# A hybrid attention and recurrence layer: the rotary key in two passes, and a smaller clearing matmul

## The chip, the cores and the metric

The kernel runs on one core of one Trainium2 chip. The metric is the device time of one execution in microseconds. Three runs of the kernel before gave 794.63, 794.14 and 793.93 us: the median is 794.14 us.

The engines are named as the profile names them: PE is the matrix engine, with PEld for its weight loads; DVE is VectorE, ACT is ScalarE, POOL is GpSimd, and SP issues most of the DMAs. Each works through its own list of instructions in order. The lists are made when the kernel is compiled, by a planner that walks the program in the order in which it is written, gives each instruction a priority by its place (moved by `prio`), and fills an engine with the ready instruction of the highest priority. So an engine's order differs in places from the order in the source.

## The reference

One layer of a diffusion backbone over 512 latent tokens and 256 context tokens, with model width 1024, all in 32-bit floats:

```python
cq, ckv, kpe, hq, hi, hg, ff, fb = split(modulate(rmsnorm(x)) @ w_in)   # for latent and for context tokens
# group A, latent attention: 4 heads, 128 plain and 64 rotary key dimensions, values of 128
k = concat([kn, apply_rope(kpe, cos, sin)])     # latent keys; one rotary key for all heads
k_ctx = concat([kn_c, kpe_c])                   # context keys: the rotary part is not turned
o_a = softmax(q @ k.T / sqrt(192)) @ v
# group B, a gated linear recurrence: 4 heads, two directions, in chunks of 64 tokens
A = where(mask, (q * exp(b - b_ref)) @ (k * exp(b_ref - b)).T, 0)       # inside a chunk
o_b = A @ v + (q * exp(b)) @ S                  # S: the state carried from chunk to chunk
x = x + gt1 * (concat([o_a, rmsnorm(o_b) * silu(hg)]) @ w_out)
x = x + gt2 * swiglu(modulate(rmsnorm(x)))      # then a last rmsnorm
```

`apply_rope` turns pairs of the 64 dimensions that lie 16 apart by an angle per token: each dimension is multiplied by a cosine, and its partner, with a sign, by a sine.

## The kernel before

**Numbers in two halves.** A matmul of two 32-bit float operands is done as three faster passes: each operand is stored as a rounded high half and the rest, a low half, and `mm3` (lines 150, 151 and 152) adds high x high, high x low and low x high in PSUM. Weights come in units of 128 x 1024 (`make_unit`): a DMA into `wf`, a cast by ACT into the high half `wh` (L132), and a subtraction by DVE into the low half `wl` (L133). There are three buffers of each, so a unit's preparation waits until PE has finished with the unit three places ahead. The halves of the normalised input are `hh`, `hl` (latent, 512 columns) and `gh`, `gl` (context, 256 columns).

**Stages.** The kernel first makes the modulation and the normalised input, with the first projection beside it. From about 100 us on come the compressed attention inputs (`mla_pass`), then for each head of the recurrence its query (`hgrn_q`) and two gates (`gates`), 8 contraction steps each through `project`. The recurrence itself (`hgrn_dir` for each head and direction, `hgrn_out` for each head) is written as generators in a list `side`; `tick()` advances the first three of them, from inside the projections, so that their small matmuls stand between the large ones. After the last head comes `mla_kpe`, which projects the rotary key, and then the attention's values (`make_v`), the rotary and plain queries (`make_qr`, `make_q`), the keys (`make_k`), the scores, the softmax and the output projection, and last the feed-forward part, which takes the second half of the time.

**The rotary key.** The weight unit holds its 64 columns twice, the second time with partners exchanged, so that one projection of 128 output rows gives the key and the exchanged key: three passes over 512 and over 256 columns in each of 8 steps. DVE multiplies the first 64 rows by the cosines (L713) and the others by the sines (L714); ACT moves the latter to the first 64 partitions (L715); DVE adds (L716). Then the high half is cast twice by ACT (L719, to both partition halves of `krh`) and the low half is subtracted twice by DVE (L720), apart for context, read from PSUM, and latent, read from `kp`.

**The chunk product.** For each head and direction, `pa` takes the product inside the chunks: a bank of 128 x 512, of which the chunks' diagonal blocks are wanted. One matmul with a weight of zeros clears the whole bank (L549). 16 small ones (L555) with 32 weight columns each, one for each group of 32 key tokens, then add into 64 or 32 columns each, leaving out the half chunks that the mask would remove. DVE copies the bank into `am` under the mask (L559); GpSimd adds the two directions (L592).

PSUM is in eight banks: two tiles `big` of two banks each (projections, `make_v`, scores) and four tiles `sm` of one. `hgrn_out` ends with matmuls into `po` (L598, L604), a norm (L610 on ACT, L614 on DVE) and transposes (L620). The states between chunks are copied by ACT (L581, L584) and chained by DVE (L585) in a low priority.

## Time and profile before

| | us |
|---|---|
| median of three runs | 794.14 |
| the profiled execution | 792.62 |
| its span, first to last instruction | 790.8 |
| PE busy | 768.1 (97%) |
| PE's weight loads | 631.7 (80%) |
| DVE busy | 446.9 (57%) |
| ACT busy | 311.4 (39%) |
| POOL busy | 10.1 (1%) |

The mean granted clock of PE is 0.988. The profile gives one execution. A matmul is shown from its start to a modelled end, and matmuls overlap in the pipeline, so the distance from one start to the next is what one costs in a row of them. In a group, the name before the arrow is the tile that is written and those behind it are read; the figure after the bar is the total in us and the mean in ns. A row of the chain of waits names the time at which a piece of it starts, its length, and the engine, tile and line. A row of waits names who waited, on whom, the total, how often and the longest.

### The profile page before, as it was taken

The numbers are of one execution on the slowest core, as the hardware profiler recorded it, in microseconds if no ns is written. First come the engines' busy times: TensorE is split into PE (matmuls) and PEld (weight loads), VectorE is DVE, ScalarE is ACT, GpSimd is POOL, SyncE is SP. The second block draws the span as 40 slices with busy tenths as digits, with TensorE's granted clock in tenths as the row PEclk, the third lists the DMA queues.
The fourth block names the chain that finished last, engine by engine and source line by source line (L and its number), as shares of the span: only waits on it lengthen the run. The fifth ranks groups of instructions, "written<-read, shape, count | busy, mean of one in ns | idle before, by whom it ended". The sixth has DMA issues, their size and how long they took to land.

```text
span 790.8 us, 10832 instructions
## 1 busy us (share of the span) xinstructions
PE 768.1 (97%) x4342; PEld 631.7 (80%) x4342; DVE 446.9 (57%) x820; ACT 311.4 (39%) x569; POOL 10.1 (1%) x18
## 2 busy tenths in 40 slices
PE   8899999999999989999999999999999999999995
PEld 7568878788887768888999888888888888888885
DVE  5576569839778989985566434432333233223324
ACT  6344246434544577664344223222322222212211
POOL 0000000000000100000000000000000000000000
PEclk8899999999999999999999999999999999999997
DMA  9923723311110022345403343423232323332303
GB/s 332 390 76 134 252 80 108 133 57 55 64 55 28 28 80 90 125 165 181 160 2 100 113 160 133 151 89 107 80 107 82 104 78 96 93 100 80 111 3 107
DMA packets 26706, 88.77 MB, mean 112 GB/s; under 512 B 2976, under 2 KB 5280, under 8 KB 26528
## 3 DMA queue, kind: packets, MB, share of 16 engines
q1 hardware_dynamic: 25568, 87.03, 33.0%
q10 hardware_dynamic: 1088, 1.05, 0.4%
q8 instruction: 34, 0.56, 0.3%
q14 instruction: 16, 0.13, 0.1%
HBM read 85.97 MB, written 2.10 MB: 111 GB/s over the span
## 4 chain that ended last, share of the span: by engine, by line
PE 89%; DVE 7%; ACT 2%; issue 1%; DMA 1%; SPq 0%; DVEq 0%; ACTq 0%
PE big L150 18%; PE big L151 17%; PE big L152 17%; PE sm L150 9%; PE sm L151 9%; PE sm L152 9%; PE big L857 2%; PE sm L604 1%; PE sm L876 1%; PE big L858 1%; PE sm L320 1%; DVE U L585 1%; PE sm L598 1%; DVE acl L309 1%; DVE G L506 1%
## 5 line engine op out<-in xcount | busy, mean ns | idle before, releaser
L133 DVE TENSOR_TENSOR wl<-wf,wh 128x1024 fp32r<-128x1024 f32 (+2 forms) x100 | 119.6, 1196 | 186.3 <-ACT wh L132 186.2
L132 ACT CAST wh<-wf 128x1024 fp32r<-128x1024 f32 (+2 forms) x100 | 102.9, 1029 | 280.3 <-PE big L151 167.6
L150 PE MATMUL big<-h2h,wh 128*128 128x512 f32 (+1 forms) x368 | 140.3, 381 | 0.0
L151 PE MATMUL big<-h2l,wh 128*128 128x512 f32 (+1 forms) x368 | 140.0, 381 | 0.0
L152 PE MATMUL big<-h2h,wl 128*128 128x512 f32 (+1 forms) x368 | 140.0, 381 | 0.0
L151 PEld LDWEIGHTS big<-h2l,wh 128*128 128x128 f32 x368 | 69.2, 188 | 14.6
L150 PEld LDWEIGHTS big<-h2h,wh 128*128 128x128 f32 x368 | 69.2, 188 | 14.4
L152 PEld LDWEIGHTS big<-h2h,wl 128*128 128x128 f32 x368 | 69.2, 188 | 14.4
L150 PE MATMUL sm<-ah,wh 128*128 128x512 f32 (+1 forms) x198 | 73.5, 371 | 0.0
L152 PE MATMUL sm<-ah,wl 128*128 128x512 f32 (+1 forms) x198 | 73.4, 371 | 0.0
L151 PE MATMUL sm<-al,wh 128*128 128x512 f32 (+1 forms) x198 | 73.4, 370 | 0.0
L427 DVE SCALAR_TENSOR_TENSOR wl<-wl,cs 128x1024 f32<-128x1024 f32 x32 | 39.0, 1220 | 33.8 <-DMA wl<-in_wmt_dram 33.8
L150 PE MATMUL big<-wh,hh 128*128 128x512 f32 x96 | 40.2, 422 | 3.3 <-ACT hh L340 1.9
L150 PEld LDWEIGHTS sm<-ah,wh 128*128 128x128 f32 x198 | 37.3, 188 | 7.1
L151 PEld LDWEIGHTS sm<-al,wh 128*128 128x128 f32 x198 | 37.3, 188 | 7.1
L152 PEld LDWEIGHTS sm<-ah,wl 128*128 128x128 f32 x198 | 37.3, 188 | 7.1
L150 PE MATMUL big<-hh,wh 128*128 128x512 f32 x104 | 42.8, 412 | 0.0
L151 PE MATMUL big<-hl,wh 128*128 128x512 f32 x104 | 40.9, 394 | 0.0
L152 PE MATMUL big<-hh,wl 128*128 128x512 f32 x104 | 40.8, 392 | 0.0
L151 PE MATMUL big<-wl,hh 128*128 128x512 f32 x96 | 38.8, 406 | 0.0
L152 PE MATMUL big<-wh,hl 128*128 128x512 f32 x96 | 38.4, 402 | 0.0
L506 DVE RECIPROCAL G<-S 128x528 f32<-128x528 f32 x8 | 27.5, 3432 | 0.1
(326 smaller groups left out, 1353.4 us busy)
## 6 DMA issues: line engine op xcount, KB each, us to landing
wf<-in_wgu_dram SPq DMA_DIRECT2D x44, 512.0 KB, 3.4
wl<-in_wmt_dram SPq DMA_DIRECT2D x32, 512.0 KB, 3.5
wf<-in_wi_dram SPq DMA_DIRECT2D x25, 512.0 KB, 3.9
wf<-in_wd_dram SPq DMA_DIRECT2D x16, 512.0 KB, 3.5
wms<-in_wm_dram SPq DMA_DIRECT2D x11, 512.0 KB, 9.6
wf<-in_wo_dram SPq DMA_DIRECT2D x8, 512.0 KB, 3.5
wf<-in_wd_dram SPq DMA_DIRECT2D x8, 384.0 KB, 3.1
wm<-in_wm_dram SPq DMA_DIRECT2D x5, 512.0 KB, 10.2
```

The lines of the kernel that those rows point to most:

```text
L132: nc.scalar.copy(hi[:, :w], f[:, :w])
L133: nc.vector.tensor_sub(lo[:, :w], f[:, :w], hi[:, :w].bitcast(F32))
L150: nc.tensor.matmul(o, lh, rh, start=start, stop=False, skip_group_check=True)
L151: nc.tensor.matmul(o, lh, rl, start=False, stop=False, skip_group_check=True)
L152: nc.tensor.matmul(o, ll, rh, start=False, stop=stop, skip_group_check=True)
L309: nc.vector.tensor_add(acc_, acc_, sq_)
L320: nc.tensor.matmul(ps[32 * g : 32 * g + 32, :256], csil[:, 4 * j + kk, :], f[:, kk * 256 : (kk + 1) * 256], start=(j == 0), stop=(j == 1), ...
L427: nc.vector.scalar_tensor_tensor(f, f, 1.0, sc, op0=ALU.mult, op1=ALU.mult, accum_out=acc)
L506: nc.vector.reciprocal(I, S)
L585: nc.vector.scalar_tensor_tensor(U[:, c1, :], U[:, c0, :], er[:, 1, c0 : c0 + 1], U[:, c1, :], op0=ALU.mult, op1=ALU.add)
L598: nc.tensor.matmul(t, a2[:, j, :], vt[:, j, h * P : (h + 1) * P], start=True, stop=False, skip_group_check=True)
L857: nc.tensor.matmul(ps[:, 0, :], L, R[:, :NL], start=(i == 0), stop=(i == 4), skip_group_check=True)
```

## The change

**The rotary key** is projected from a unit with only its 64 columns, half as wide (512 instead of 1024 columns for each partition). The unit's high half and low half are written side by side into one tile, 64 columns of each for every contraction step, so that one pass gives the product with the high half in the first 64 output rows and with the low half in the other 64. There are two passes for each step, with the high and the low half of the input; the product of the two low halves, which was left out before, is now in the sum. Afterwards ACT moves the lower 64 rows to the first 64 partitions, DVE adds them over all 768 columns, exchanges the partners by a shuffle, and multiplies and adds; casts and subtractions then take latent and context columns together. The tile `kp` uses the buffers of `kk` instead of those of `q`.

**The chunk product** is no longer cleared as a whole. Two matmuls of zeros in bfloat16, with 32 weight columns and 128 moving columns, clear only the corners of the diagonal blocks that the small matmuls don't write; the small matmuls now write instead of adding. The masked copy is done in two operations of 64 partitions, for the diagonal blocks alone.

```diff
-        units.append(("wi", wi[u], UNIT))
+        units.append(("wi", wi[u], UNIT) if u < NW_IN - 1 else ("kp", wi[u][:, : UNIT // 2], UNIT // 2))
...
-        nc.scalar.copy(hi[:, :w], f[:, :w])
-        nc.vector.tensor_sub(lo[:, :w], f[:, :w], hi[:, :w].bitcast(F32))
+        if kind == "kp":
+            f3 = f[:, :w].rearrange("p (k c) -> p k c", c=64)
+            h3 = hi.rearrange("p (k s c) -> p k s c", s=2, c=64)
+            nc.scalar.copy(h3[:, :, 0], f3)
+            nc.vector.tensor_sub(h3[:, :, 1], f3, h3[:, :, 0].bitcast(F32))
+        else:
+            nc.scalar.copy(hi[:, :w], f[:, :w])
+            nc.vector.tensor_sub(lo[:, :w], f[:, :w], hi[:, :w].bitcast(F32))
...
-    zr = HG.tile([P, P], F32R, name="zr")
-    nc.gpsimd.memset(zr.bitcast(F32), 0.0)
+    zr = HG.tile([P, P], F32, name="zr")
+    nc.gpsimd.memset(zr, 0.0)
     zc = zr.bitcast(BF16)
...
         pa = sm()
-        nc.tensor.matmul(pa, zr, hh[:, 0, :], start=True, stop=False, skip_group_check=True)
+        for g in (1 - d, 3 - d):
+            c0 = (g // 2) * CH + 32 * d
+            nc.tensor.matmul(pa[32 * g : 32 * g + 32].rearrange("p (j t) -> p j t", t=P)[:, :, c0 : c0 + 32],
+                             zc[:, 0:32], zc[:, 0:P].rearrange("p (j t) -> p j t", t=32), start=True, stop=True,
+                             skip_group_check=True, tile_position=(0, 32 * g))
...
-                                 start=False, stop=True, skip_group_check=True, tile_position=(0, 32 * g))
+                                 start=True, stop=True, skip_group_check=True, tile_position=(0, 32 * g))
         with prio(100):
             p4 = pa.rearrange("p (j t) -> p j t", t=P)
-            nc.vector.copy_predicated(am[d], mk[:, d : d + 1, :].to_broadcast([P, 4, P]), p4)
+            for g in range(2):
+                r = slice(g * CH, (g + 1) * CH)
+                nc.vector.copy_predicated(am[d][r, :, r], mk[r, d : d + 1, r].to_broadcast([CH, 4, CH]), p4[r, :, r])
...
     def mla_kpe():
-        ps = project(KPU)
-        kp = HG.tile([P, NL], F32, tag="q", name=nm("kp"), bufs=2)
-        m = HG.tile([P, NL], F32, tag="sg", name=nm("kpm"), bufs=2)
-        nc.vector.tensor_mul(kp[0:64, :], ps[0:64, :NL], C("cos")[0:64, :])
-        nc.vector.tensor_mul(kp[64:128, :], ps[64:128, :NL], C("sin")[64:128, :])
-        nc.scalar.copy(m[0:64, :], kp[64:128, :])
-        nc.vector.tensor_add(kp[0:64, :], kp[0:64, :], m[0:64, :])
-        for src, c in ((ps[0:64, NL:NT], slice(NL, NT)), (kp[0:64, :], slice(0, NL))):
-            for r in (slice(0, 64), slice(64, 128)):
-                nc.scalar.copy(krh[r, c], src)
-                nc.vector.tensor_sub(krl[r, c], src, krh[0:64, c].bitcast(F32))
+        w, _ = unit(KPU)
+        ps = big()
+        for k in range(KT):
+            for i in range(2):
+                for o, n, t in ((ps[:, 0, :], NL, (hh, hl)), (ps[:, 1, :NC], NC, (gh, gl))):
+                    nc.tensor.matmul(o, w[:, k * P : (k + 1) * P], t[i][:, k, :n], start=(k == 0 and i == 0),
+                                     stop=(k == KT - 1 and i == 1), skip_group_check=True)
+            if k in (1, 4):
+                tick()
+        ps = ps.rearrange("p a b -> p (a b)")
+        kp = HG.tile([P, NT], F32, tag="kk", name=nm("kp"), bufs=3)
+        m = HG.tile([P, NT], F32, tag="sg", name=nm("kpm"), bufs=2)
+        nc.scalar.copy(m[0:64, :], ps[64:128, :NT])
+        nc.vector.tensor_add(kp[0:64, :], ps[0:64, :NT], m[0:64, :])
+        nc.vector.stream_shuffle(m[0:64, :NL], kp[0:64, :NL], SWAP)
+        nc.vector.tensor_mul(kp[0:64, :NL], kp[0:64, :NL], C("cos")[0:64, :])
+        nc.vector.tensor_mul(m[0:64, :NL], m[0:64, :NL], C("sin")[0:64, :])
+        nc.vector.tensor_add(kp[0:64, :NL], kp[0:64, :NL], m[0:64, :NL])
+        for r in (slice(0, 64), slice(64, 128)):
+            nc.scalar.copy(krh[r, :], kp[0:64, :])
+            nc.vector.tensor_sub(krl[r, :], kp[0:64, :], krh[0:64, :].bitcast(F32))
```

The host packs the last unit with the 64 columns alone and zeros behind them; a second definition of the shuffle's table is dropped.

6 lines of the change are left out of this document (2 added, 4 removed).

## The prediction

> **What bounds the kernel now.** I read the page's first part, then the stretches, the waits of TensorE (PE), the chain of waits, and the timeline of the place where the rotary key is made.
>
> ```profile
> PE 768.1 (97%) x4342; PEld 631.7 (80%) x4342; DVE 446.9 (57%) x820; ACT 311.4 (39%) x569; POOL 10.1 (1%) x18
> ```
>
> Read alone, this row says that every matmul taken out is time won. The stretches say where this isn't so (columns: PE, weight loads, VectorE, ScalarE and GpSimd busy, clock, DMA).
>
> ```profile
> 210.00:230.00 20.00, 20.00 (x156) 16.43 (x155) 17.04 (x41) 8.12 (x19) 0.00 (x0) 1.00 0.09 29
> 264.00:276.00 12.00, 10.35 (x84) 7.75 (x83) 11.64 (x22) 7.51 (x18) 3.57 (x4) 1.00 0.13 46
> 288.00:300.00 12.00, 9.85 (x50) 7.64 (x50) 11.09 (x22) 11.25 (x17) 0.00 (x0) 1.00 0.24 82
> 360.00:400.00 40.00, 40.00 (x250) 35.89 (x249) 21.69 (x37) 16.16 (x26) 0.00 (x0) 1.00 0.40 130
> ```
>
> Up to 230 us and from 360 us on PE never rests, so a shift is kept to the end. Where the rotary key lies, around 264 to 300 us, VectorE (DVE) is nearly full (11.64 of 12) and PE has holes. The longest of PE's waits there, and the chain, name them:
>
> ```profile
> PE big L150 <- DVE krl L720: 1.6, 1, 1.6
> ```
>
> ```profile
> 231.76 1.05 ACT wh L132
> ...
> 237.35 0.62 DVE am L559
> ...
> 251.44 0.70 DVE qg L531
> ...
> 264.97 0.59 DVE kp L713
> ...
> 270.96 0.50 PE big L150
> ...
> 281.92 0.37 PE sm L604 x4
> ...
> 293.51 0.30 PE sm L620
> ```
>
> From 251.44 to 270.96 us the chain is DVE's alone; PE restarts at 270.96 when DVE has read the rotary key's PSUM for the last time (L720). Then PE leads to the last head's output (L604), whose transposes (L620) follow at 293.51.
>
> **The change: PE's part of the rotary key.** One step of its contraction, and a clearing matmul behind it:
>
> ```profile
> 252.88 0.40 PE L150 MATMUL big<-hh,wh 128*128 128x512 f32 x1
> 253.11 0.40 PE L151 MATMUL big<-hl,wh 128*128 128x512 f32 x1
> ...
> 253.58 0.28 PE L150 MATMUL big<-gh,wh 128*128 128x256 f32 x1
> 253.70 0.28 PE L151 MATMUL big<-gl,wh 128*128 128x256 f32 x1
> ...
> 253.93 0.39 PE L549 MATMUL sm<-hh,zr 128*128 128x512 f32 x1
> 254.25 0.65 PE L555 MATMUL sm<-qt,kk 128*32 128x64 f32 x32
> 254.83 0.50 PE L150 MATMUL big<-hh,wh 128*128 128x512 f32 x1
> 255.17 0.39 PE L151 MATMUL big<-hl,wh 128*128 128x512 f32 x1
> ```
>
> Matmuls overlap, so the price is the distance between starts: 0.23 us for a pass over 512 latent columns, 0.12 for 256 context columns, 1.05 for the step of three passes. Two passes leave out one of each in eight steps: 8 x 0.35 = 2.8 us of PE. The weight's own preparation (half the load, half a cast, half a subtraction) falls in the stretch from 210 to 230 us, where PE's other projections keep it busy 20.00 of 20.00 us; I cost it at nothing. Without that cover it would gain half of such a subtraction, 0.6 us by the row of L133 further down.
>
> **The clearing.** L549 takes 0.32 us to the next start here. After other small matmuls it takes more:
>
> ```profile
> 227.09 0.60 PE L544 MATMUL sm<-cs,kk 128*128 128x128 f32 x4
> 227.44 0.47 PE L549 MATMUL sm<-hh,zr 128*128 128x512 f32 x1
> 227.85 0.65 PE L555 MATMUL sm<-qt,kk 128*32 128x64 f32 x32
> ```
>
> That is 0.41 us. What replaces it, two bfloat16 matmuls with 32 weight columns over 128 moving columns, is in no row. From below, L555: 32 records in 0.58 us, so 0.04 for two. From above, a matmul right behind one of another kind: 254.83 to 255.17 is 0.34 where 0.23 is usual; two of those are 0.68. The nearest row is L544, 128 columns, four in 0.35: 0.18 for two. With fewer weight columns I take 0.15, an estimate. Saved: about 0.25 each (from 0.37 down to a loss of 0.27), 2.0 for all eight. Five come before 231.76, where the chain leaves PE for ScalarE (ACT) and DVE: 1.25 us. The sixth is beside the chain; the last two lie in DVE's stretch. The accumulating matmuls that now start afresh have the same shapes: nothing.
>
> By the Trainium skill, "TensorE: Matmul & The Clock Gate", section "Back-to-back issue gap", 128 columns are 134 cycles, 0.056 us, and matmuls in different column groups overlap; each clearing would then save 0.35 and the first five 1.75 instead of 1.25. No run here shows it yet.
>
> **VectorE.** The groups, shapes kept apart (mean ns last before the bar):
>
> ```profile
> L713 DVE TENSOR_TENSOR kp<-big,cs 64x512 f32<-64x512 f32 x1 | 0.7, 675 | 0.0
> L714 DVE TENSOR_TENSOR kp<-big,cs 64x512 f32<-64x512 f32 x1 | 0.7, 694 | 0.0
> L716 DVE TENSOR_TENSOR kp<-kp,kpm 64x512 f32<-64x512 f32 x1 | 1.4, 1416 | 0.0
> L720 DVE TENSOR_TENSOR krl<-big,krh 64x256 fp32r<-64x256 f32 x2 | 0.8, 412 | 0.0
> L720 DVE TENSOR_TENSOR krl<-kp,krh 64x512 fp32r<-64x512 f32 x2 | 1.4, 685 | 0.0
> L786 DVE STREAM_SHUFFLE m<-sm 128x512 f32<-128x512 f32 x2 | 1.5, 732 | 0.0
> L861 DVE TENSOR_REDUCE ast<-big 128x1 f32<-128x768 f32 x1 | 1.0, 958 | 0.4 <-PE big L858 0.4
> L559 DVE COPY_PREDICATED am<-mk,sm 128x512 f32<-128x512 int32 x8 | 5.7, 710 | 0.0
> ```
>
> The rotary key costs DVE 0.68 + 0.69 + 1.42 + 2 x 0.41 + 2 x 0.69 = 4.98 us. Afterwards: one add over 768 columns (0.96, as L861), a shuffle (0.73), two products and an add over 512 (3 x 0.69), two subtractions over 768 (2 x 0.96): 5.68. The masked copy becomes two of 256 columns at about 0.41 each (as L720): 0.13 more each time, once on the chain at 237.35 and twice behind it. So DVE's list between 251 and 297 us grows by 0.70 + 0.26 = 0.96 us. The 1.42 of L716 is twice what its size asks (L714: 0.69). It ran beside this row:
>
> ```profile
> 267.18 1.27 POOL L592 TENSOR_TENSOR a<-am,am 128x512 f32<-128x512 f32 x1 [27.58 <-DVE am L559]
> ```
>
> GpSimd's add ends at 268.45 and L716 at 269.00. I credited the removal of the whole 1.42, so if one of the new operations meets that add, up to 1.27 comes on top: from 0 to 1.27, I take 0.35, half the excess seen.
>
> The Trainium skill, "SBUF — State Buffer", section "SBUF: two separate sides", says a DVE operation with two SBUF inputs and a GpSimd operation that reads SBUF exclude each other for a whole instruction; it speaks against this change, whose products and last add are all of that kind. L716 bears it out: blocked to 268.45, then 0.55. By the rule alone the list grows by 0.96 + 0.73 = 1.69.
>
> **ScalarE.** The rotary key took five copies, three over 512 columns (0.62, first row) and two over 256, at most 3.1 us. Now there are three over 768, 0.81 each by the sigmoid of that size:
>
> ```profile
> 269.03 0.62 ACT L719 CAST krh<-kp 64x512 fp32r<-64x512 f32 x1 [1.36 <-DVE kp L716]
> 270.58 0.27 ACT L581 COPY U<-sm 128x128 f32<-128x128 f32 x1
> L470 ACT ACTIVATE sg<-big 128x768 f32<-128x768 f32 x8 | 6.4, 806 | 0.0
> ```
>
> 2.4 us; the gain of up to 0.7 is on an engine busy 7.51 of 12 us and costs or gives nothing. The new first copy makes DVE's add wait; queued behind it is DVE's whole list, but PE delivers 2.8 us sooner, so the copy finds ACT and PSUM ready by the time DVE reaches L713's place at 264.97.
>
> **Where the stall goes.** The key's PSUM is now read out by that one add, some 5 us ahead of 270.96, so PE's 1.64 us wait at 270.96 goes. What is late next is DVE's list up to the last head's states (for L604, 281.92) and to the `ow` that L620 transposes. DVE's own gaps from 279 to 297 are
>
> ```profile
> 278.99 0.69 DVE L803 TENSOR_TENSOR vl<-big,vh 128x512 fp32r<-128x512 f32 x1 [0.56 <-ACT vh L802]
> 281.18 1.23 DVE L133 TENSOR_TENSOR wl<-wf,wh 128x1024 fp32r<-128x1024 f32 x1 [0.38 <-ACT wh L132]
> 287.01 0.17 DVE L191 TENSOR_SCALAR rsv<-oss 128x4 f32<-128x4 f32 x1 [0.46 <-ACT osq L610]
> 287.50 0.69 DVE L776 SCALAR_TENSOR_TENSOR qnl<-big,qnh 128x512 fp32r<-128x512 f32 x1 [0.32 <-ACT qnh L775]
> ```
>
> 1.72 us, all behind work that waits for PE; a PE some 4 us ahead can close them. A weight subtraction like the one at 281.18, 1.23 us, can also be left until after the first scores; I count half of it, 0.6.
>
> **Sum.** -1.25 (five clearings) + 0.13 (masked copy on the chain) = -1.12 at 251.44. Then +0.96 + 0.35 (DVE's list) - 1.72 (gaps) - 0.6 = -1.01. Together -2.1 us: the profiled execution goes from 792.62 (790.8 of span and 1.8 around it) to 790.5. The median of the three runs is 794.14, 1.5 above the profiled one; on it the forecast is **792.0**. Of 4.8 us of PE work removed, less than half arrives.
>
> **Rivals.**
> 1. *All of PE's saving arrives.* For it: PE's 97%, and the instruction order is planned anew, so DVE's less urgent work may move past 300 us. Against: DVE 11.64 of 12 us busy from 264 to 276. -4.8: 789.3.
> 2. *DVE swallows the key's saving.* The gaps stay, because all four rows name ACT as what ended them, the block recurs in full: -1.12 + 0.96 + 0.73 = +0.6, less half a subtraction left until later (0.6) and 0.2 of the gaps: -0.2, so 793.9. For it: the chain is DVE's from 251 to 271. Against: the copies that ACT waited on come from PE, which is now ahead.
> 3. *Slower: the states queue behind the longer key.* On ACT the casts of the key stood at 269.03, ahead of the states' copy at 270.58, in order. From L713's place at 264.97 the new chain needs 0.96 + 0.73 + 3 x 0.69 = 3.8 us, with masked copies (0.82) and a full block (1.27) 2.1 more: 270.9 instead of 269.0. With two casts 0.19 longer each the states start 2.3 later; less the 1.12, +1.2: 795.3. It decides once the new last add ends over 1.12 us after 269.0 and PE has nothing else to put before L604. Against: the planner can issue the states first.
> 4. *The change doesn't do what it says:* if the corner pair cost 0.68, five clearings lose 1.35; it moves forecast and rival 2 up by 2.6. I count it within rivals 2 and 3.
>
> **Numbers.** Forecast 0.50, own range 790.8 to 793.2 (clearing 0.1 to 0.35 each, block 0 to 1.27); all of PE 0.17; swallowed 0.23; slower 0.10. A change below 0.2%, 1.6 us, can't be told from none: the line lies at 792.55. Forecast gives four fifths to faster, rival 1 all: 0.57. Slower, beyond 795.7, is a little under half of rival 3 and the tail of rival 2: 0.06. The rest, 0.37, is same. The range runs from rival 1's price to just under rival 3's: 789.3 to 794.9.
>
> **What would show it.** Right: 16 matmuls fewer of L150 to L152's kind in the key, its span from 8.4 to 5.6 us of matmuls; the clearing pair at about 0.15 us; no PE wait of 1.6 us on the key's PSUM; DVE still over 95% busy from 264 to 276; L620 at about 291.4. Wrong: L620 near 289 (rival 1) or at 293 and later (rival 2), the states' first copy on ACT after 271 (rival 3), or a clearing pair at 0.4 us or more.

## The result, and the profile after

The changed kernel takes 800.81 us (median of 4 runs, 799.62 to 801.84) against 794.05 of the kernel before: ratio 1.0083, 95% interval 1.0065 to 1.0101. It is slower, by some 6.8 us, where 2.1 us less were forecast. The profiled execution took 799.62 us, with a span of 797.8.

Line numbers shift: L150 to L152 are now L156 to L158, the states' links L585 are L597, the weighted heads L614 are L626, their transposes L620 are L632, the first scores L857 are L877. First the row of busy times from the page's first part, and TensorE's longest waits around the rotary key, with one from further up, on `shg` (total, times, longest):

```profile
PE 766.2 (96%) x4334; PEld 629.3 (79%) x4334; DVE 450.7 (56%) x829; ACT 311.9 (39%) x567; POOL 10.7 (1%) x18
```

```profile
PE sm L632 <- DVE ow L626: 5.3, 1, 5.3
PE big L877 <- ACT pp L883: 2.5, 1, 2.5
PE sm L156 <- ACT U L596: 1.8, 1, 1.8
...
PE big L156 <- DVE shg L650: 1.0, 1, 1.0
...
PE big L156 <- DVE kp L733: 0.9, 1, 0.9
```

PE lost exactly the instructions it was to lose (4342 - 16 key passes + 8 second corner matmuls = 4334), and the 1.6 us wait on the key's PSUM fell to 0.9. But PE now waits 5.3 us for the last head's weighted heads, where it waited 1.2 us in the kernel before, and 2.5 us for the first exponentials.

Four marks divide the span: the decayed queries `qg` of the last head's first direction (the queries times their decay, `q * exp(b)` of the reference), the weighted heads `ow` (the last head's output under its norm and gate), the first scores, the end. For the kernel before, two of them had no row yet (timeline: start, duration, engine, line, operation):

```profile
293.02 1.12 DVE L614 SCALAR_TENSOR_TENSOR ow<-sm,rsr,shg 128x128 f32<-128x128 f32 x4
296.80 0.39 PE L857 MATMUL big<-knh,qnh 128*128 128x512 f32 x1
```

and for the changed kernel:

```profile
250.71 0.69 DVE L537 TENSOR_TENSOR qg<-qt,S 128x512 f32<-128x512 f32 x1 [2.74 <-PE sm L616]
295.65 1.13 DVE L626 SCALAR_TENSOR_TENSOR ow<-sm,rsr,shg 128x128 f32<-128x128 f32 x4
301.97 0.40 PE L877 MATMUL big<-knh,qnh 128*128 128x512 f32 x1
```

| stretch, us | before | after | difference |
|---|---|---|---|
| start to `qg` | 251.44 | 250.71 | -0.73 |
| `qg` to `ow` | 41.58 | 44.94 | +3.36 |
| `ow` to first scores | 3.78 | 6.32 | +2.54 |
| first scores to the end of the span | 494.0 | 495.8 | +1.8 |

All of the loss lies behind `qg`. The 0.73 us before it are not the change's. The transposes in front of the first clearing, up to which both kernels do the same work, already start 1.06 us apart (before, then changed):

```profile
129.33 0.38 PE L539 MATMUL sm<-cs,kk 128*128 128x128 f32 x2
128.27 0.38 PE L545 MATMUL sm<-cs,kk 128*128 128x128 f32 x2
```

In the first 60 us the profile of the kernel before has a granted clock of 0.91, that of the changed kernel 0.94: 10.2 and 6.8 us at half clock. Two profiles in which the order is the old one up to here, before and before_sqrt_late further down, differ in the same way: 10.2 and 3.4 us at half clock, and the first clearing at 129.91 and 128.22. From these transposes to `qg` the changed kernel took 122.44 us, the kernel before 122.11.

**From `qg` to `ow`.** VectorE's timeline of the changed kernel, from the key's first add (L733) to the last link of the states (L597):

```profile
262.66 0.95 DVE L733 TENSOR_TENSOR kp<-big,kpm 64x768 f32<-64x768 f32 x1
...
266.35 0.90 DVE L571 COPY_PREDICATED am<-mk,sm 64x256 f32<-64x256 int32 x2 [1.06 <-PE sm L565]
267.28 0.68 DVE L735 TENSOR_TENSOR kp<-kp,cs 64x512 f32<-64x512 f32 x1
267.89 1.77 DVE L736 TENSOR_TENSOR kpm<-kpm,cs 64x512 f32<-64x512 f32 x1
...
272.09 1.91 DVE L740 TENSOR_TENSOR krl<-kp,krh 64x768 fp32r<-64x768 f32 x2
...
275.89 1.21 DVE L139 TENSOR_TENSOR wl<-wf,wh 128x1024 fp32r<-128x1024 f32 x1
...
282.04 0.68 DVE L796 SCALAR_TENSOR_TENSOR qnl<-big,qnh 128x512 fp32r<-128x512 f32 x1
...
285.01 0.33 DVE L597 SCALAR_TENSOR_TENSOR U<-U,er 128x128 f32<-128x128 f32 x1
```

In the kernel before, the key's last subtractions and the last link of the states were these:

```profile
270.94 1.38 DVE L720 TENSOR_TENSOR krl<-kp,krh 64x512 fp32r<-64x512 f32 x2
...
280.46 0.35 DVE L585 SCALAR_TENSOR_TENSOR U<-U,er 128x128 f32<-128x128 f32 x1
```

GpSimd's row beside L736 in the changed kernel:

```profile
267.42 1.69 POOL L604 TENSOR_TENSOR a<-am,am 128x512 f32<-128x512 f32 x1 [28.53 <-DVE am L571]
```

The last link of the states ends at 285.34, 34.6 us after `qg`; in the kernel before it ended at 280.81, 29.4 us after. Of these 5.3 us, 2.4 are there when the key is done: its last subtraction ends 23.3 us after `qg`, in the kernel before 20.9. There the key's longer work on VectorE and the wait of 1.06 us up to 266.35 count. The other 2.9 us come behind the key, from the order. Ten links stand in the list there, each a third of a microsecond, where the kernel before had eight, and between them stand a weight subtraction, value and query splits (the subtractions that make the low halves `vl`, `qnl`) and rotary products; in the kernel before, the weight subtraction came behind the last link and no query split in front of it. PE's parts of these end sooner in the planned order, which presumably is why the planner put them in front of links that decide more.

**From `ow` to the scores, and behind.** The stretches (PE, weight loads, VectorE, ScalarE and GpSimd busy, clock, DMA):

```profile
292.00:294.00 2.00, 0.00 (x0) 0.00 (x0) 1.53 (x3) 1.97 (x4) 0.00 (x0) 0.78 0.74 236
294.00:296.00 2.00, 0.00 (x0) 0.00 (x0) 1.90 (x7) 1.97 (x4) 0.00 (x0) 0.50 0.86 258
296.00:298.00 2.00, 1.85 (x7) 1.59 (x8) 1.76 (x5) 1.96 (x3) 0.00 (x0) 0.50 0.22 82
298.00:300.00 2.00, 2.00 (x8) 1.61 (x7) 1.94 (x3) 1.97 (x4) 0.00 (x0) 0.52 0.00 0
300.00:304.00 4.00, 4.00 (x25) 3.51 (x24) 2.51 (x6) 2.56 (x5) 0.00 (x0) 1.00 0.45 131
...
310.00:312.00 2.00, 2.00 (x12) 1.86 (x10) 1.78 (x6) 0.69 (x3) 0.00 (x0) 0.54 0.46 121
312.00:314.00 2.00, 2.00 (x9) 1.76 (x8) 1.54 (x5) 1.77 (x5) 0.00 (x0) 0.60 0.37 141
```

During the 5.3 us wait the granted clock falls to one half. A stretch of 2 us at clock c holds (1 - c) x 4 us of half clock: 0.88 + 2 + 2 + 1.92 = 6.8 us, then 1.84 + 1.60 = 3.4 us after the wait for the exponentials. The kernel before has none between 240 and 340 us:

```profile
240.00:340.00 100.00, 94.52 (x623) 76.65 (x623) 90.20 (x186) 65.62 (x143) 3.57 (x4) 1.00 0.23 76
```

PE worked from 296.15 (the end of the wait) to about 299.9 at half clock, which loses it half of 3.8 us, and through the second fall, half of 3.4: 1.9 and 1.7 us of PE's work. The second is nearly all of the +1.8; how much of the +2.54 the first is, these rows don't say.

ScalarE adds a piece: the square root that is meant to warm its table for the end of the kernel (L1057) had been planned this early, and in the changed order its table load stands ahead of the casts of the nope key (`knh`, the plain part of the keys, which is not turned):

```profile
299.74 1.28 ACT L1057 ACT_TABLE_LOAD   x1
...
301.14 1.50 ACT L788 CAST knh<-sm 128x512 fp32r<-128x512 f32 x3
...
306.36 1.28 ACT L883 ACT_TABLE_LOAD   x1 [3.72 <-DVE ast L881]
```

In the kernel before the first nope-key casts started at 296.06 and this load at 297.88, behind them.

### The profile page after: what moved, and what is told of

It reads as the page before. It is cut to its first block, busy times and chain, and to the rows that moved or that the text cites. A ratio compares the mean times of both kernels' runs of the same rounds, so it can differ in the third digit from the quotient of the medians.

```text
span 797.8 us, 10824 instructions
## 1 busy us (share of the span) xinstructions
PE 766.2 (96%) x4334; PEld 629.3 (79%) x4334; DVE 450.7 (56%) x829; ACT 311.9 (39%) x567; POOL 10.7 (1%) x18
## 4 chain that ended last, share of the span: by engine, by line
PE 80%; DVE 9%; DMA 5%; ACT 3%; issue 2%; SPq 0%; DVEq 0%; ACTq 0%
PE big L156 16%; PE big L157 15%; PE big L158 15%; PE sm L156 9%; PE sm L157 9%; PE sm L158 9%; PE big L877 2%; DMA wl<-in_wmt_dram 1%; DMA xc<-in_ctxT_dram 1%; PE sm L896 1%; PE sm L616 1%; DVE wl L139 1%; DMA wm<-in_wm_dram 1%; DMA wms<-in_wm_dram 1%; PE big L878 1%
## 5 line engine op out<-in xcount | busy, mean ns | idle before, releaser
L139 DVE TENSOR_TENSOR wl<-wf,wh 128x1024 fp32r<-128x1024 f32 (+1 forms) x99 | 118.4, 1196 | 186.6 <-ACT wh L138 186.5
L138 ACT CAST wh<-wf 128x1024 fp32r<-128x1024 f32 (+1 forms) x99 | 101.8, 1029 | 276.5 <-PE big L157 162.5
L156 PE MATMUL big<-h2h,wh 128*128 128x512 f32 (+1 forms) x368 | 140.3, 381 | 0.0
L158 PE MATMUL big<-h2h,wl 128*128 128x512 f32 (+1 forms) x368 | 140.0, 381 | 0.0
L158 PEld LDWEIGHTS big<-h2h,wl 128*128 128x128 f32 x368 | 69.2, 188 | 14.4
L156 PEld LDWEIGHTS big<-h2h,wh 128*128 128x128 f32 x368 | 69.2, 188 | 14.4
L156 PE MATMUL sm<-ah,wh 128*128 128x512 f32 (+1 forms) x198 | 73.5, 371 | 0.0
L158 PE MATMUL sm<-ah,wl 128*128 128x512 f32 (+1 forms) x198 | 73.4, 371 | 0.0
L156 PE MATMUL big<-wh,hh 128*128 128x512 f32 x96 | 39.4, 414 | 4.3 <-ACT hh L346 1.9
L156 PEld LDWEIGHTS sm<-ah,wh 128*128 128x128 f32 x198 | 37.3, 188 | 7.1
L158 PEld LDWEIGHTS sm<-ah,wl 128*128 128x128 f32 x198 | 37.3, 188 | 7.1
L156 PE MATMUL big<-hh,wh 128*128 128x512 f32 x96 | 39.4, 410 | 0.0
L158 PE MATMUL big<-wh,hl 128*128 128x512 f32 x96 | 38.2, 399 | 0.0
L157 PE MATMUL big<-hl,wh 128*128 128x512 f32 x96 | 37.8, 394 | 0.0
L158 PE MATMUL big<-hh,wl 128*128 128x512 f32 x96 | 37.7, 393 | 0.0
L156 PEld LDWEIGHTS big<-wh,hh 128*128 128x128 f32 x96 | 17.9, 188 | 12.5 <-ACT hh L346 3.6
```

What stands on the lines that cost most here:

```text
L138: nc.scalar.copy(hi[:, :w], f[:, :w])
L139: nc.vector.tensor_sub(lo[:, :w], f[:, :w], hi[:, :w].bitcast(F32))
L156: nc.tensor.matmul(o, lh, rh, start=start, stop=False, skip_group_check=True)
L157: nc.tensor.matmul(o, lh, rl, start=False, stop=False, skip_group_check=True)
L158: nc.tensor.matmul(o, ll, rh, start=False, stop=stop, skip_group_check=True)
```

## The experiments

Theory A, formed from this profile: the last head's chain, threaded through queues in the planner's order, sets this stretch; the change altered that order for the worse, and PE's saving became waits. Rival, called C further on: the new parts cost by themselves, whatever the order. The letters of the expectations are not always these: for clear_only and key_only, A is the key's longer work and B the order; for the two runs with the late square root, A is that table loads lie on the chain and B that they hide in waits. All ratios are to the kernel before, run on the same chip beside it. The last three columns are read from one profiled execution each, as above.

| kernel | ratio (95%) | `qg` to `ow` | `ow` to scores | half clock, 240 to 340 |
|---|---|---|---|---|
| before | 1 | 41.6 | 3.8 | 0 |
| the whole change | 1.0083 (1.0065 to 1.0101) | 44.9 | 6.3 | 10.2 |
| clear_only | 1.0013 (0.9993 to 1.0033) | 41.8 | 6.0 | 3.4 |
| key_only | 1.0056 (1.0034 to 1.0078) | 42.4 | 7.1 | 6.8 |
| two_passes_old_chain | 1.0115 (1.0086 to 1.0143) | 42.8 | 9.3 | 10.2 |
| three_passes_new_chain | 1.0066 (1.0031 to 1.0101) | 42.7 | 7.3 | 6.8 |
| states_first | 1.0054 (1.0034 to 1.0075) | 41.3 | 6.8 | 6.8 |
| before_states_first | 1.0065 (1.0033 to 1.0097) | 43.4 | 7.8 | 6.8 |
| key_after_head1 | 1.0157 (1.0133 to 1.0181) | 42.5 | 6.0 | 13.6 |
| filled_wait | 1.0055 (1.0036 to 1.0075) | 44.9 | 4.6 | 3.4 |
| after_sqrt_late | 1.0055 (1.0028 to 1.0081) | 44.9 | 4.7 | 3.4 |
| before_sqrt_late | 1.0003 (0.9979 to 1.0027) | 41.6 | 3.8 | 0 |
| chain_first | 1.0072 (1.0045 to 1.0098) | 34.8 | 14.9 | 3.4 |
| before_chain_first | 1.0043 (1.0020 to 1.0066) | 37.7 | 10.3 | 3.4 |
| loads_late | 1.0168 (1.0134 to 1.0202) | 46.3 | 4.6 | 6.8 |
| before_loads_late | 1.0103 (1.0081 to 1.0125) | 41.6 | 3.2 | 0 |
| chain_first_loads_late | 1.0112 (1.0087 to 1.0136) | 38.7 | 11.3 | 10.2 |
| before_chain_first_loads_late | 1.0093 (1.0061 to 1.0124) | 37.7 | 6.5 | 0 |
| filled_sqrt_late | 1.0054 (1.0032 to 1.0076) | 46.3 | 4.6 | 3.4 |
| filled_sqrt_late_states_mid | 1.0041 (1.0017 to 1.0065) | 42.2 | 7.0 | 3.4 |

**One part alone.** clear_only is the kernel before with the diff's parts in `hgrn_dir` and `zr`; key_only the kernel before with all the others.

> Only the corner clearing and the two masked copies; the rotary key as before. Theory A (the loss comes from the key: its longer work on VectorE and ScalarE holds up the last head's states): the clearing saves about 0.2 us each, so 792 to 793.5 us, PE waits for ow about 1.2 us as before. Theory B (any change of PE's pace makes the planner put the last head's states later on VectorE): slower than before, 795 to 799, with a PE wait for ow of over 3 us.

> Only the rotary key in two passes; the old clearing of the whole bank. Theory A: 800 to 802.5 us, the whole loss and 1 us of clearing more, PE waits about 5 us for ow. Theory B: slower too, but by any amount between 796 and 802, since the planner's order is another one again.

Clearing alone makes no difference that can be measured, though PE waits 2.6 us for `ow` with it (1.2 before), which neither expectation had; the key alone costs 0.56%, with a wait of 4.7 us, inside B's range and under A's. GpSimd's block did not recur in key_only, so the key is slower without it too (the product that took 1.77 us above):

```profile
270.17 0.76 DVE L729 TENSOR_TENSOR kp<-kp,cs 64x512 f32<-64x512 f32 x1
270.86 0.68 DVE L730 TENSOR_TENSOR kpm<-kpm,cs 64x512 f32<-64x512 f32 x1
```

Then the key's two halves, PE's passes and VectorE's chain, each without the other:

```diff
 two_passes_old_chain, against before (with the new clearing)
-        ps = project(KPU)
...
+            for i in range(2):   # hh x wh and hl x wh, hh x wl left out
+                for o, n, t in ((ps[:, 0, :], NL, (hh, hl)), (ps[:, 1, :NC], NC, (gh, gl))):
+                    nc.tensor.matmul(o, L[0], t[i][:, k, :n], ...)
...
 three_passes_new_chain, against the whole change
-            for i in range(2):
+            for i in (0, 1, 1):
```

> The new clearing, the old weight layout and the old VectorE work for the rotary key, but only two of its three passes (the product of the input's high half with the weight's low half is left out): PE's saving alone. If the longer VectorE work is the cause of the loss: 791.5 to 793.5. If PE's saving itself turns into a wait, with a halved clock behind it: 795 to 799, with PE waiting for ow over 3 us.

> The whole change with a third pass in the rotary key (the input's low half counted twice): VectorE's new work alone, PE as before. If the longer VectorE work is the cause: 799 to 802. If it takes PE's saving to bring about the loss: 793 to 796.

Both are slower than before, and the one with PE's saving and the old, shorter VectorE chain is likely the slower of the two (the intervals overlap a little). PE's saving by itself brought no gain: it came back as waits of 2.6 us for the third head's `ow`, 2.8 for the nope key and 2.2 for the exponentials, with 10.2 us of half clock. Its median of 803.3 is above both expectations. The other run, with 798.5, lies just under the 799 to 802 that were given for VectorE's longer work as the cause: the new chain, beside a PE that has as much to do in the key as before, is enough for most of the loss. That speaks for C; but the order is another one there too.

**The order alone.** The links of the last head's states have priority -100 in the planner; states_first and before_states_first make it +100, in the changed kernel and in the kernel before:

```diff
-        with prio(-100):
+        with prio(100 if h == NH - 1 else -100):
             U = HG.tile([P, NCH, P], F32, tag="U", name=nm("U"), bufs=2)
```

> The whole change, and the last head's state chain (ScalarE's copies and VectorE's links) planned 100 places earlier instead of 100 later. If the states' place in the queues is the cause: no PE wait for ow above 2 us, the last head's output matmuls start before 281 us instead of at 285.8, no clock below 0.95 between 288 and 300 us, 789 to 792.5 us. If it is the amount of work on VectorE (rotary key 5.7 us and the block by GpSimd): the wait moves to another place and the time stays at 798 to 801.

> The kernel before with the same priority for the last head's states and nothing else. If the states' place is the cause of the loss only in the changed kernel: 792.5 to 794.5, since they stood well there already. If the old kernel lost time by it too (its waits of 1.6 and 1.2 us): 790 to 792.5.

With the priority the states ended 23.3 us after `qg` in the changed kernel, 11.3 us sooner, and `ow` came only 3.6 us sooner: PE's output products stood behind value products in PE's order. The time stayed at 799.5 and the waits moved (1.8 us for `onl`, 2.2 for the exponentials), which is what was expected if the amount of VectorE's work is the cause. The same one-line edit makes the kernel before 0.65% slower with nothing else changed, against both of its expectations. So an order alone, with the same work, moves the time by nearly as much as this change did. That is the strongest row for theory A. key_after_head1 moves the key out of the stretch (and its weight unit with it):

```diff
...
-    mla_kpe()
+        if h == 1:
+            mla_kpe()
+            tick()
     tick()
```

> The whole change, and the rotary key projected after the second head (its weight unit moved in the list), where VectorE has slack, instead of after the last one. If the amount of work that VectorE has between 251 and 300 us sets the time: that stretch (from the last head's qg to the first scores, 45.4 us before, 51.3 in the changed kernel) falls to 40 to 43 us plus nothing elsewhere, 788 to 791.5 us. If it is only the order that the planner happens to choose: the stretch minus PE's key work stays over 43, and the time is anywhere from 793 to 800.

It is the slowest but one, and its time lies outside both expectations (the stretch to the scores is 48.5 us). Without the key PE has less to do beside the last head's chain; it waits 6.4 us for `ow` and 5.3 us for a value split and has four windows of half clock. `qg` to `ow` stays at 42.5: work taken from PE here is not time won.

**The clock.** In filled_wait PE multiplies 128 x 128 ones (22 products) in the wait for `ow`; no result uses them, and the order of the instructions up to there is that of the changed kernel.

```diff
+        rr0 = sq
...
         pt = sm()
+        if h == NH - 1:
+            with prio(0):
+                for _ in range(22):
+                    nc.tensor.matmul(pt[:, :P], ones, rr0, start=True, stop=True, skip_group_check=True)
         for j in range(4):
             nc.tensor.transpose(pt[:, j * P : (j + 1) * P], w[:, j, :], ident)
```

> The whole change, with 22 idle matmuls (ones times an old tile, the result overwritten) put in front of the last head's transposes, where PE waited 5.3 us for ow. The engines' orders are those of the changed kernel up to that place, so the wait itself stays. If PE's halved clock after the wait is part of the loss: clock 1.00 from 290 to 300 us, passes 0.23 us apart instead of 0.43 behind the transposes, the first scores 1.5 to 2 us earlier than in the changed kernel, 798.5 to 799.5. If the slow clock costs nothing because ScalarE and VectorE set the pace there: 800 to 801.5.

```profile
288.00:300.00 12.00, 11.73 (x82) 10.03 (x83) 10.47 (x21) 11.12 (x22) 0.00 (x0) 1.00 0.38 132
300.00:320.00 20.00, 17.87 (x103) 15.77 (x102) 15.48 (x31) 13.29 (x26) 0.00 (x0) 0.91 0.26 80
```

The clock stays at 1.00 through the wait, `ow` to scores falls from 6.3 to 4.6 us, and the ratio from 1.0083 to 1.0055; the intervals of the two ratios overlap. The fall behind the first scores stays (0.91). But the clock is not all that changed. Behind the fillers the planner put the square root's table load behind the nope key's casts, where the changed kernel had it in front:

```profile
298.89 1.37 ACT L793 CAST knh<-sm 128x512 fp32r<-128x512 f32 x3
300.28 1.28 ACT L1062 ACT_TABLE_LOAD   x1
```

So this run can't say what the half clock in the wait was worth: the 1.7 us may be the load's. The next run, after_sqrt_late, takes the load out and keeps 3.2 us of half clock behind the wait, and its first scores come nearly as soon after `ow` (4.7 us). What it loses is other work of PE: up to the first scores it has done 6 passes over 512 columns of the key projection, filled_wait 12, a difference of 1.4 us at 0.23 each.

The mean granted clock of every run is on record, and says more than one profile. The ten runs of filled_wait have 0.9886 on average, those of the kernel before beside them 0.9879, and filled_wait is still 4.5 us slower on average: that much is lost without any more half clock than the kernel before has. In key_only the means are 0.9830 and 0.9879. Within the runs of the kernel before, 0.01 of clock goes with 7 to 8 us, so the clock would be some 3.8 of key_only's 5.0 us, and with 0.9848 against 0.988 some 2.5 of the changed kernel's 6.8; both are estimates.

**Table loads.** Two runs make the warm-up square root read the last tile of the feed-forward product, so that it can't be planned early:

```diff
-    nc.scalar.activation(epst2, epst, AF.Sqrt)
+    nc.scalar.activation(epst2, al[:, FT - 1, 0:1].bitcast(F32), AF.Sqrt, scale=0.0, bias=epst)
```

> The whole change; the square root that warms its table for the end of the kernel (L1057) reads the last tile of the feed-forward product, so that its 1.28 us table load and the reload of the exponential's table leave the stretch ahead of the first scores. Computes the same result. Theory A (loads on the chain): the first nope-key casts no longer stand behind the load at 299.74, and the exponential no longer behind a reload; last weighted heads to first scores 6.3 -> about 4.5 us, time 800.8 -> 797 to 798.5. Still slower than before, because the states' detour (44.9 us from the last decayed queries to the weighted heads, against 41.6) stays. Theory B (loads hide in waits): no difference over 0.5 us.

> The kernel before with the same late square root. Theory A: before has its load behind the first nope-key cast, so only the exponential's reload goes, 1.3 us at most: 792.5 to 793.7 beside 794.0. Theory B: no difference. With the run above it says how much of the 6.8 us is the place of a table load: the difference of the two gains, 1 to 3 us by A, 0 by B.

In the changed kernel the casts now follow the output's copy at once and the reload of the exponential's table is gone:

```profile
299.05 0.67 ACT L634 ACTIVATE onh<-sm,vc 128x512 fp32r<-128x512 f32 x1
299.69 1.08 ACT L788 CAST knh<-sm 128x512 fp32r<-128x512 f32 x2
304.70 0.90 ACT L883 ACTIVATE pp<-big,ast 128x768 f32<-128x768 f32 x1 [3.93 <-DVE ast L881]
```

Scores 1.6 us sooner, the first exponential 3.0 us sooner (304.70 against 307.65), and the wait that had halved the clock a second time is gone. 1.0055 instead of 1.0083, as expected; the intervals overlap here too. In the kernel before the profile has the first exponential 1.3 us sooner after `qg` (49.2 us against 50.5), which the times, at 0.9979 to 1.0027, can't show.

**The whole chain ahead.** chain_first gives priority +100 not only to the states but to the last head's output products, norm, weighted heads and transposes, with the late square root; before_chain_first does the same to the kernel before.

```diff
+        with prio(100 if h == NH - 1 else 0):
             po = sm()
             for j in range(4):
             ...
+        with prio(100 if h == NH - 1 else 0):
             pt = sm()
             for j in range(4):
                 nc.tensor.transpose(pt[:, j * P : (j + 1) * P], w[:, j, :], ident)
             ...
```

> The whole change with the late square root, and the last head's states, output products, norm, weighted heads and their transposes given priority in the planner (+100), so that the tail of this head no longer stands behind the value and query splits of the attention in VectorE's and TensorE's queues. Computes the same result. Theory A (the last head's chain in the planner's order sets this stretch, and the change lengthened it): the weighted heads come before the last query products, at 33 to 38 us after the last decayed queries instead of 44.9; TensorE then has no wait over 2 us up to the first scores and no half clock, so the stretch to the first scores falls from 51.3 to 43 to 46 us (TensorE's own work there is 41.9), and the time to 789 to 793, faster than before. Theory C (the new parts cost by themselves, whatever the order): still 3 us or more slower than the kernel below.

> The kernel before with the same late square root and the same priorities. Theory A: its stretch to the first scores was 45.4 us with 45.1 of the engines' work threaded well, and TensorE has about 4 us more to do here than in the kernel above (8 x 0.35 us of key passes and the fp32 clearings), so 44 to 48 us and 791 to 795, and the whole change with chain_first is 1 to 4 us faster than this one: the saving that was predicted shows once the chain is out of the way. Theory C: this one is 3 us or more faster than the kernel above.

`ow` came 10 us sooner after `qg` in the changed kernel, as theory A said, and the time did not follow: 1.0072 and 1.0043, where A had both at or under the kernel before, and the changed one ahead. It is behind by less than C asked (3 us). What is late next stands on ScalarE and in PE's wait for it:

```profile
293.53 1.28 ACT L836 ACT_TABLE_LOAD   x1
294.83 1.06 ACT L836 ACTIVATE scs<-cs 128x1024 f32<-128x1024 f32 x1
295.79 0.58 ACT L797 ACTIVATE qnh<-big 128x512 fp32r<-128x512 f32 x1
296.39 1.28 ACT L840 ACT_TABLE_LOAD   x1
...
298.73 1.61 ACT L790 CAST knh<-sm 128x512 fp32r<-128x512 f32 x4
```

```profile
299.36 0.79 PE L879 MATMUL big<-knh,qnh 128*128 128x512 f32 x1 [4.41 <-ACT knh L790]
```

The sigmoid of the conditioning vector and two table loads, which the long wait for `ow` had hidden, now set the scores. The next four runs move these too: the sigmoid behind the last exponential, the exponential's warm-up behind the first nope-key casts.

```diff
-    nc.scalar.activation(scs, scx, AF.Sigmoid)
-    nc.vector.tensor_mul(scx, scx, scs)
-    nc.scalar.activation(epst2, scs[:, 0:1], AF.Exp)
     ...
     make_k(0)
+    nc.scalar.activation(epst2, knh[:, 0, NT - 1 : NT].bitcast(F32), AF.Exp, scale=0.0)
     ...
+    for a in (0, 512):   # after the loop over the heads' tiles
+        ...
+        nc.scalar.activation(scs, scx[:, a : a + 512], AF.Sigmoid)
+        nc.vector.tensor_mul(scx[:, a : a + 512], scx[:, a : a + 512], scs)
     wps.append(wout_a(1))
```

> The whole change with all of ScalarE's table work taken out of the stretch ahead of the first scores: the square root's warm-up late as before, the second sigmoid of the conditioning vector (L834) after the last exponential, and the exponential's warm-up after the first nope-key casts. Computes the same result. Theory A (TensorE's saving is lost to waits that ScalarE and VectorE put on the way to the first scores): the scores start 3 to 5 us sooner than in the changed kernel (46 to 48 us after the last decayed queries, against 51.3), and the time is 794 to 797 beside 794.0 of before, since the states' detour stays. Theory C (the new parts cost by themselves): 797 or more.

> The kernel before with the same three moves. Its loads stood in the wait for the last head's weighted heads (sigmoid and exponential loads at 291.23 and 294.08 beside weighted heads at 293.02), so Theory A expects little: the reload of the exponential's table and the warm-up, 1 to 2 us, 792 to 793.5.

> The whole change with the priorities of the run chain_first and the three moves of the run loads_late. In chain_first the weighted heads came 10 us sooner but TensorE then waited 4.4 us for the nope key, which stood behind two table loads, a sigmoid and a weight cast on ScalarE (293.53 to 298.73). Theory A: with these gone that wait falls under 1.5 us, the first scores come 44 to 46 us after the last decayed queries (51.3 in the changed kernel, 45.4 in before), and the time is 789 to 793. Theory C: 795 or more.

> The kernel before with the priorities of chain_first and the three moves. Theory A: TensorE's own work decides here, which is 3 to 4 us longer than in the run above, so this one is 1 to 4 us slower than it: 791 to 795. Theory C: it is 3 us or more faster than the run above.

Theory A's times failed in all four. C's bounds were met by the two changed kernels; with the priorities the kernel before is 2.5 us ahead where C asked for 3. But most of the loss has a reason outside the stretch. The kernel before with late loads reaches its scores in 44.8 us (45.4), and then loses it:

```profile
PE sm L150 <- ACT rh L132: 4.0, 1, 4.0
```

Between 360 and 400 us PE waits for the first output weight, and 6.8 us of half clock follow; all four of these kernels have such a wait there, of 4.0 to 4.6 us, and the half clock. Presumably it comes because the conditioning products that need the sigmoid now come all at once, and their weights share staging buffers and DMA with the output's (a DMA share of 0.75 there, 0.40 in the kernel before). Of the stretch itself they still tell something. With priorities and late loads the kernel before takes 44.2 us to the scores without any half clock; the changed kernel 50.0 us, of which this stands in it:

```profile
276.00:278.00 2.00, 2.00 (x20) 1.44 (x18) 1.97 (x4) 0.00 (x0) 1.55 (x2) 0.73 0.30 119
278.00:286.00 8.00, 8.00 (x25) 4.89 (x22) 2.88 (x7) 2.69 (x10) 0.73 (x1) 0.50 0.21 66
286.00:288.00 2.00, 2.00 (x8) 1.57 (x7) 2.00 (x7) 1.44 (x3) 0.00 (x0) 0.71 0.00 0
```

10.2 us of half clock after a wait of 1.9 us, with PE busy throughout: up to 5.1 us of the 5.8 us difference.

**Do the terms add?** filled_sqrt_late joins the fillers and the late square root; filled_sqrt_late_states_mid adds priority +50 for the last head's states.

> The whole change with the 22 idle products of the run filled_wait (in TensorE's wait for the last head's weighted heads) and the late square root of the run after_sqrt_late. Computes the same result. Alone each took about 0.28% off the changed kernel's ratio to before (1.0083 -> 1.0055). If the half clock after the wait and the table load are two separate terms of the loss, they add: ratio 1.002 to 1.004, and what is left is the states' detour. If they are one and the same 2 us (a load that only counts because the clock is low), 1.005 or more.

> The run above, and the last head's states at priority +50 instead of -100 (+100 was the run states_first), which in VectorE's order puts their links ahead of the value splits but leaves the key's operations where they are. If the states' detour (44.9 us from the last decayed queries to the weighted heads) is the third term of the loss: that stretch falls to 40 to 42 us, the ratio to 0.997 to 1.001, so no slower than before. If any change of the order costs, as in states_first: 1.004 or more.

They don't add: 1.0054, the same as either alone. That is no wonder for the load, which filled_wait had already moved behind the nope key. The wait for `ow` was filled, but now the 1.8 us wait on the states' copies, which had cost no clock in the changed kernel, halved it from 271.6 to 275.0, and `qg` to `ow` grew from 44.9 to 46.3 us. With the states in between, that stretch fell to 42.2 us and `ow` to scores rose to 7.0. No kernel of these beats the kernel before.

**What follows.** Between the marks, the +7.0 us of span of the profiled execution divide into -0.7 ahead of `qg`, +3.4 for the states' detour, +2.5 from `ow` to the first scores and +1.8 behind. The first is not the change's, as said above. The second is shown by rows; states_first took it back in its stretch and still ended at 1.0054. Of the third, 1.6 us went with the table load. The fourth goes with the second fall of the clock. That the detour would be the rest, so that the three together bring the change to no loss, was expected and did not come.

Between kernels with the same priorities and loads, the changed one stands against the old one, in per cent of the time: +0.83 as they are, +0.52 with the late square root, +0.29 with the chain first, +0.65 and +0.19 with late loads, -0.11 with the states first. The first is uncertain by 0.2, the others by some 0.3 to 0.4 each. All five others are below 0.83, which suggests that a good part of it belongs to order, loads and clock and not to the new parts. How large that part is, and whether the new parts are worth anything of their own, stays open. A changed kernel without any wait of PE over 1.7 us in this stretch was not found.

## Why the prediction was wrong

*PE's key passes.* Right: 16 matmuls fewer, and the key's last pass starts 10.4 us after `qg` instead of 12.1, with a stall of 1.2 us on the transposes inside it.

*The clearing.* Right on PE, but the term of the sum failed:

```profile
252.19 0.28 PE L725 MATMUL big<-gl,wh 128*128 128x256 f32 x1
252.40 0.23 PE L557 MATMUL sm<-zr 128*32 128x128 bf16 x2
252.41 0.65 PE L565 MATMUL sm<-qt,kk 128*32 128x64 f32 x32
```

After a context pass the next start is due 0.12 us later, at 252.31; the masked products start at 252.41, so the pair costs 0.10 us (0.15 taken, 0.32 for the old matmul there). In the first five places, from the first of the six transposes in front to the first masked product, it was 0.98 us and is 0.76: 0.22 saved by each, where 0.25 was taken, so with 0.41 for the old matmul the pair costs some 0.19 there. By the Trainium skill ("TensorE: Matmul & The Clock Gate", section "Back-to-back issue gap", with the overlap of different column groups from its part on packing small matmuls) the pair would take about 0.06, an estimate; the 0.10 lies between that and the 0.15 taken, the 0.19 above both.

The forecast's first term, -1.12 at `qg`, took it that this time arrives there. It did not: from the transposes at 128.27 to `qg` the changed kernel took 0.33 us more than the kernel before. PE, being ahead, ran into a wait that the kernel before doesn't have, 1.04 us up to 153.17 for VectorE's product `shg` (L650). That `qg` stands 0.73 us sooner in the profile is luck of the clock at its start.

*VectorE's list.* Six rows of the key (the last of two operations) took 0.95, 0.71, 0.68, 1.77, 0.67 and 1.91, together 6.69 us; 5.68 + 0.35 was taken. The masked copies took 0.90 where 0.82 was taken. The block term is the one mis-sized: L736 took 1.77 beside GpSimd's 1.69 where the same shape took 0.68 in key_only, 1.09 too much. I had taken a third of that. By the Trainium skill ("SBUF — State Buffer", section "SBUF: two separate sides") the second of two such operations is blocked until the first has ended; the trace agrees: GpSimd's add ended at 269.11 and L736 0.55 us later, as L716 did in the kernel before.

*"Where the stall goes".* This step failed. It closed VectorE's gaps (-1.72), let half a subtraction go behind the scores (-0.6), and kept the order in which VectorE would take its list. The stall on PSUM did shrink, but a PE that is ahead doesn't only close gaps. Less urgent work, a weight subtraction included, stands in front of the links in the new order, presumably because PE made it ready sooner, and the states ended 5.3 us later relative to `qg`: 2.4 by the key's longer list and a wait in it, 2.9 by the order behind it. VectorE was 10.82 of 12 us busy from 264 to 276, not over 95%; a masked copy waited 1.06 us there for products that PE had put behind other matmuls.

*What no step had.* The clock. The forecast valued a PE wait at its own length. The sum has no term for the half clock behind it (3.6 us of PE's work in this profile; some 2.5 us by the mean clock of the runs), and none for a table load that moves to the wrong side of the nope key.

*The rivals.* Rival 3, slower, was right in sign and in its place, wrong in its mechanism and size. Its mark, the states' first copy after 271, did not come:

```profile
267.85 0.27 ACT L593 COPY U<-sm 128x128 f32<-128x128 f32 x1 [1.07 <-PE sm L588]
...
271.06 1.69 ACT L739 CAST krh<-kp 64x768 fp32r<-64x768 f32 x2 [1.01 <-DVE kp L737]
272.76 0.63 ACT L596 ACTIVATE U<-sm,er 128x128 f32<-128x128 f32 x2
```

Only the last two copies queued behind the key's casts on ScalarE; the links queued on VectorE. It had 795.3 as its price because it, too, stopped at the states. Rival 2, with PE's saving swallowed by VectorE, described `qg` to `ow` best, and had no term for it going beyond zero. The range ended at 794.9, just under rival 3's price; with a planner that orders the whole program anew, it should have been open upwards.

## What to carry to other kernels

Where the instruction order is planned, cutting work from an engine that has waits in a stretch changes the order there, and the order is a larger term (0.65% here for one priority) than the few microseconds cut: price the chain of the latest result through each queue again, and allow for a loss. In these profiles a wait of TensorE past 1.7 us could bring 3.4 us or more at half clock behind it, which is 1.7 us of TensorE's work for each 3.4; past 2.4 us each did. So count such a wait at more than its length. A table load in idle time is free only as long as the idle time stays where it is. After such a change look first at the longest new wait and the clock of its stretch, then at the totals, and compare two profiles by the distance between marks, not by a mark's time from the start. And before an experiment is read as a test of one thing, look whether the planner has moved another with it, as it moved the table load in filled_wait.

## What was not expected of the hardware

Half clock came in whole windows of 3.4 us: in all twenty kernels the sum between 240 and 340 us, by the 2 us stretches, is 0, 3.4, 6.8, 10.2 or 13.6. In that stretch PE waits up to 1.69 us never had one behind them; from 2.47 us on each had; in between both occur (1.77 without in the changed kernel and with in filled_sqrt_late, 1.92 without in chain_first and with in chain_first_loads_late, 2.25 without in states_first). One wait of 5.3 us brought two windows in the changed kernel and, in the same order of instructions up to its end, one in after_sqrt_late, starting at 296.0 instead of 293.1. The Trainium skill ("TensorE: Matmul & The Clock Gate", section "What's actually happening") has half clock after an idle window of about 3.4 us, counted in windows that run free of the kernel; the length and the free phase agree with these rows, but waits of half that length, from 1.76 us on, sufficed here. No single threshold comes out of the rows, and in chain_first_loads_late the half clock lasted three windows with PE busy all the while.

The windows also lie differently at the start of each execution. In the first 60 us the twenty profiles have between 3.4 and 20.5 us of half clock, and their first clearing starts anywhere from 127.5 to 134.9 us, though the work up to there is the same. The runs spread accordingly: the kernel before took 789.0 to 798.1 us in 31 runs on one chip, with mean clocks from 0.994 down to 0.982, some 7 us for 0.01, while its one profile has the clock under 1 only at the start and the end. The rows with ten runs have intervals of 0.19 to 0.32% to either side, so a difference of 2 us (0.25%) needs about that many of each kernel, or a comparison of profiles by stretches.
